# New durations and an overlap rule for the planner that orders the engines' work in a two-layer hybrid attention trunk

## The chip, the core and the metric

The kernel runs on one core of one Trainium2 chip. Its engines are TensorE (PE in the profile, with its weight loads as PEld), VectorE (DVE), ScalarE (ACT), GpSimd (POOL) and SyncE (SP), which issues nearly all transfers. Each engine takes its instructions in the order in which the program lists them and waits at an instruction until what it needs is there. The metric is the device time of one execution in microseconds: a median of 625.37 us over three runs (625.07 to 625.52) for the kernel before.

## The reference, cut to what matters

The input is 256 rows of 1024 numbers. Each of two layers normalises the rows, projects them through one matrix of 9808 columns, runs three causal attentions of 8 heads of 64 on slices of the projection, multiplies each by a SiLU gate, projects each back to 1024 channels, merges the three by sigmoid gates, projects once more and adds the residual. A last normalisation follows.

```python
for layer in range(2):
    h = rms_norm(x, gain[layer])
    proj = h @ w_in[layer]              # q, k, v, gate for a, b, c; indexer; forget; merge logits
    oa = moba(rope(qa), rope(ka), va) * silu(ga)       # one block of 256: plain causal softmax
    ob = dsa(rope(qb), rope(kb), vb, top 64 keys by the indexer) * silu(gb)
    oc = forgetting(qc, kc, vc, log_sigmoid(f)) * silu(gc)
    y = [oa @ w_branch[0], ob @ w_branch[1], oc @ w_branch[2]]
    x = x + sum(sigmoid(merge[n]) * y[n] for n in range(3)) @ w_out[layer]
out = rms_norm(x, final_gain)
```

All numbers are float32.

## The kernel before

**Tiling.** For float32 accuracy each operand of a matrix product is split into a high and a low part, and a product is three: high by high, low by high, high by low. A weight piece arrives by a transfer into one of three `raw` buffers. ACT copies it rounded into a `wh` buffer (L365), DVE writes the rest into a `wl` buffer (L369); there are six of each. `hTh` and `hTl` are the split normalised input. A projection unit (`unit_b`, `unit_y`) is 24 or 12 matmuls of 128x256 at L410, given to PE in groups of six, into one of three PSUM banks named `proj`. Units are named after their slice: `ga2` is the gate of pair 2 of attention a, `m06` a merge logit, `y04` a branch projection. A bank is free again when DVE and ACT have read it.

**Attention by pairs of heads.** Four pairs per attention. Queries are split and copied between the halves of the partitions (`qh`, `qx`, `qy`, L400 to L401 and L582); keys are written into a block layout (`bd`, L740, L742 and L744), one head in each half of the partitions. These half-height operations touch 64 partitions. Scores (L595, L597) go into two banks `s`; DVE adds the mask and takes the maximum (L656), ACT exponentiates (L660), DVE or ACT normalises (L671 or L668), PE transposes (L683), ACT and DVE split (L686, L688), PE multiplies with the values into the one bank `o` (L700 to L705), ACT and DVE add up the halves of it, again at half height (L720, L722), and gate and split the result into `og` (L725, L400, L401). In a layer the attentions run in the order a, c, b, between the projections of the gates and branches; the branch units `y0`, `y2`, `y1` read `og` of a, c and b. The output units `o00` to `o11` end the layer.

**What sets the order.** The kernel first only lists its operations, each with the operations that it depends on, the buffers that it needs, a key (its place in the layer) and a duration in nanoseconds for each engine that may run it. `Plan.run` then plays them through: it takes the engine whose next operation could start first, and of the operations that could start there at that very time the one with the lowest key, books the duration and emits it. So the order on each engine, and for some operations the engine (`normalise`, the product with the gate, the sum into `acc`), follow from the booked durations and from the delays between engines. On the chip the order is fixed; only the waits are real. Before the change a dependency over engines costs a delay from the table `LAG`, a half-height operation is booked with 18 ns (ACT copies) or 95 ns more than a full one, and DVE operations with two SBUF inputs are kept apart from GpSimd's for the whole of both.

## Time and profile before

| what | value |
|---|---|
| median of three runs | 625.37 us (625.07 to 625.52) |
| span of the profiled execution | 623.2 us |
| PE busy | 609.3 us (98%), 4808 matmuls |
| DVE busy | 537.7 us (86%) |
| ACT busy | 455.7 us (73%) |
| POOL busy | 90.2 us (14%) |
| granted TensorE clock | 0.998 |
| DMA queue q1, share of 16 engines | 52.3% |

The span is the time from the first to the last instruction of one profiled execution; the median lies 2.2 us above it. Successive matmuls overlap: the record of a matmul of 256 columns lasts 0.28 us while the next starts 0.11 us after it. A timeline row gives start, duration, engine, line, operation, tiles and, in brackets, idle time before it with the engine and tile that ended it.

### The profile page before, as it was taken

The page shows a single profiled execution, that of the slowest core. Times are in us where ns is not written, and L with a number is a line of the kernel's source. Part 1 is how long each engine was busy: PE and PEld are TensorE (multiplying, and loading weights), DVE is VectorE, ACT ScalarE, POOL GpSimd, SP SyncE. Part 2 cuts the span into 40 slices and gives each one's busy share as a digit, 9 for nine tenths or more (in the row PEclk, how much of TensorE's full clock was granted, in tenths as well). Part 3 has the DMA queues.
Part 4 walks back from the last instruction along what each step waited for, and adds up shares of the span by engine and source line. Part 5 has one row for each costly group of instructions (what it writes and reads, how often), then busy time and mean ns, then how long its engine had stood idle before and what let it go on. Part 6 is the DMA issues. An engine that isn't in the chain of part 4 may idle for free.

```text
span 623.2 us, 12650 instructions
## 1 busy us (share of the span) xinstructions
PE 609.3 (98%) x4808; PEld 583.7 (94%) x4808; DVE 537.7 (86%) x1320; ACT 455.7 (73%) x953; POOL 90.2 (14%) x98
## 2 busy tenths in 40 slices
PE   8999999999999999999999999999999999999995
PEld 7999999999998999999889999998999999999985
DVE  8899999975998789988689999998588977999683
ACT  5779499676986669955487867995689856987641
POOL 1243131000000223200005304200000013221001
PEclk9999999999999999999999999999999999999999
DMA  8945543686363653356655646447636364424831
GB/s 290 301 151 189 172 142 108 204 257 212 127 204 102 210 164 97 113 183 224 219 179 162 202 129 195 141 164 252 206 101 217 122 201 149 159 72 133 271 101 67
DMA packets 96155, 107.31 MB, mean 172 GB/s; under 512 B 4576, under 2 KB 84832, under 8 KB 96096
## 3 DMA queue, kind: packets, MB, share of 16 engines
q1 hardware_dynamic: 95808, 106.13, 52.3%
q8 instruction: 37, 0.61, 0.4%
q10 hardware_dynamic: 288, 0.39, 0.2%
q14 instruction: 22, 0.18, 0.1%
HBM read 103.37 MB, written 1.05 MB: 168 GB/s over the span
## 4 chain that ended last, share of the span: by engine, by line
PE 66%; ACT 16%; DVE 14%; issue 3%; POOL 0%; POOLq 0%; ACTq 0%
PE proj L410 57%; ACT wh L365 5%; DVE wl L369 4%; PE t L683 2%; ACT e L660 2%; ACT qx L582 2%; DVE isc L847 2%; PE proj L993 1%; DVE t L846 1%; ACT qy L582 1%; PE s L595 1%; PE s L597 1%; ACT pth L686 1%; PE t L908 1%; ACT ot L720 1%
## 5 line engine op out<-in xcount | busy, mean ns | idle before, releaser
L410 PE MATMUL proj<-hTh,wh 128*128 128x256 f32 (+1 forms) x1040 | 271.7, 279 | 2.7 <-DVE g L624 2.0
L369 DVE TENSOR_TENSOR wl<-raw,wh 128x1024 fp32r<-128x1024 f32 (+1 forms) x190 | 236.6, 1252 | 39.6 <-ACT wh L365 38.8
L410 PE MATMUL proj<-hTl,wh 128*128 128x256 f32 (+1 forms) x1040 | 270.1, 277 | 0.0
L365 ACT ACTIVATE wh<-raw 128x1024 fp32r<-128x1024 f32 (+1 forms) x190 | 199.0, 1055 | 70.9 <-PE proj L410 58.1
L410 PE MATMUL proj<-hTh,wl 128*128 128x256 f32 (+1 forms) x1040 | 235.1, 279 | 0.8 <-DVE wl L369 0.8
L410 PEld LDWEIGHTS proj<-hTh,wh 128*128 128x128 f32 (+1 forms) x1040 | 194.8, 187 | 3.8 <-DVE g L624 2.4
L410 PEld LDWEIGHTS proj<-hTl,wh 128*128 128x128 f32 (+1 forms) x1040 | 194.8, 187 | 0.3
L410 PEld LDWEIGHTS proj<-hTh,wl 128*128 128x128 f32 (+1 forms) x1040 | 175.7, 187 | 1.2 <-DVE wl L369 1.2
L460 POOL TENSOR_TENSOR rsh<-rsh,cst 128x256 f32<-128x256 f32 (+1 forms) x42 | 33.2, 790 | 384.8 <-DVE rsh L459 383.9
L462 POOL TENSOR_TENSOR rr<-rr,rsh 128x256 f32<-128x256 f32 (+1 forms) x42 | 48.9, 1166 | 10.0 <-DVE rr L461 6.2
L660 ACT ACTIVATE e<-e,st 128x128 f32<-128x128 f32 x96 | 42.6, 446 | 2.2 <-DVE st L656 2.0
L410 PE MATMUL proj<-wh,v 128*128 128x512 f32 (+1 forms) x144 | 35.5, 368 | 0.0
L410 PE MATMUL proj<-og0l,wh 128*128 128x256 f32 x128 | 33.9, 277 | 0.0
L410 PE MATMUL proj<-og0h,wh 128*128 128x256 f32 x128 | 32.6, 279 | 0.0
L410 PE MATMUL proj<-wh,hTh 128*128 128x512 f32 x80 | 31.8, 398 | 0.0
L410 PE MATMUL proj<-wh,hTl 128*128 128x512 f32 x80 | 31.3, 392 | 0.0
L410 PEld LDWEIGHTS proj<-wh,v 128*128 128x128 f32 x144 | 25.2, 188 | 4.7
L410 PE MATMUL proj<-og0h,wl 128*128 128x256 f32 x128 | 28.7, 277 | 0.0
L688 DVE TENSOR_TENSOR ptl<-t,pth 128x384 fp32r<-128x384 f32 x48 | 26.3, 554 | 0.9 <-ACT pth L686 0.4
L410 PE MATMUL proj<-wl,hTh 128*128 128x512 f32 x80 | 24.9, 391 | 0.0
L410 PEld LDWEIGHTS proj<-og0l,wh 128*128 128x128 f32 x128 | 24.0, 188 | 0.0
L410 PEld LDWEIGHTS proj<-og0h,wh 128*128 128x128 f32 x128 | 24.0, 188 | 0.0
(195 smaller groups left out, 1059.5 us busy)
## 6 DMA issues: line engine op xcount, KB each, us to landing
raw<-in_w_in_dram SPq DMA_DIRECT2D x74, 1024.0 KB, 5.0
raw<-in_w_branch_dram SPq DMA_DIRECT2D x24, 512.0 KB, 3.5
raw<-in_w_out_dram SPq DMA_DIRECT2D x8, 1024.0 KB, 7.0
tmp<-wf SPq DMA_DIRECT2D x16, 128.0 KB, 5.7
raw<-in_w_in_dram SPq DMA_DIRECT2D x3, 512.0 KB, 7.0
x<-in_x_dram SPq DMA_DIRECT2D x4, 256.0 KB, 4.5
raw<-in_w_in_dram SPq DMA_DIRECT2D x2, 320.0 KB, 6.5
out_dram<-tmp SPq DMA_DIRECT2D x2, 320.0 KB, 2.5
```

Of the source, the lines that this page charges most:

```text
L365: ACT.activation(p[0].v, sel(c.v), AF.Copy)
L369: DVE.tensor_tensor(p[1].v, sel(c.v), p[0].v.bitcast(F32), op=ALU.subtract)
L410: PE.matmul(o(), a(), b(), start=first and i == 0, stop=last and i == n - 1)
L460: gps(lambda: POOL.tensor_tensor(T(sh)[:np_], T(sh)[:np_], s[:np_], op=ALU.mult), S, [k_rope], [sh], key, "rope")
L462: gps(lambda: POOL.tensor_tensor(T(r)[:np_], T(r)[:np_], T(sh)[:np_], op=ALU.add), S, [sh], [r], key, "rope")
L582: act(lambda t=t, o=o, a=a, b=b: ACT.activation(T(t)[o], T(a)[b].bitcast(F32), AF.Copy), S, False, [a], [q[2]] if i is None else [kx[i]], ...
L595: PE.matmul(o.rearrange("p (h c) -> p h c", h=2), qh[:, sl], kl[:, :, :n], start=True, stop=False)
L597: PE.matmul(o[:, h * n:(h + 1) * n], x[h][:, sl], kh[:, 0 if shared else h, :n], start=False, stop=h == 1)
L660: act(lambda t=t, a=a, n=n, e=e, st=st: ACT.activation(T(e)[:, a:a + n], T(e)[:, a:a + n], AF.Exp, bias=T(st)[:, t:t + 1], scale=-1.0, acc ...
L683: PE.transpose(T(ps)[:, i * 128:(i + 1) * 128], T(es[h])[:, i * 128:(i + 1) * 128], ident)
L688: dve(lambda h=h, src=src: DVE.tensor_tensor(T(pl)[:, h], src(), T(ph)[:, h].bitcast(F32), op=ALU.subtract), 384, [ps, kp[h][0]], [kp[h][1 ...
L847: dve(lambda o=o, t8=t8: DVE.match_replace(o, T(t8), o, TAKEN), n, [t8], [k_isc[i]], key + r * step, "top8")
```

## The change

The planner's model is replaced; no operation of the kernel is added, removed or resized. Its parts:

- The table `LAG` and the constant `SEM` go. An operation counts as done 95 ns (ACT) or 85 ns (DVE) after the end of its booking, and another engine sees it 33 ns (POOL: 79 ns) after that, or 200 ns after its end if it ran on PE.
- A half-height operation no longer has a surcharge. Instead, neither it nor the operation after it may start before the one ahead on the same engine is done, plus 24 ns.
- A GpSimd operation is booked with 735 ns and 78 ns behind it (before 250 + 2.2 ns per column, 813 ns at 256); a DVE operation that shares its port may start 138 ns before GpSimd's end, and the other way round.
- A matmul of 256 columns is booked with 113.3 ns (114.8), of 512 with 231 ns (228); five bookings of small groups on PE are set anew.

```diff
+    def seen(d, e):
+        if d.eng == e == "PE":
+            return d.end
+        if d.eng == "SP":
+            return d.done + d.lag
+        return d.done + (1500.0 if e == "SP" else 200.0 if d.eng == "PE" else 79.0 if e == "POOL" else 33.0)
...
+                    if e in last and (o.half or last[e].half):
+                        tt = max(tt, last[e].done + STEP)
...
-                        tt = max(tt, d.end + d.lag + LAG.get((d.eng, e), 0.0 if d.eng == e else SEM) + (0.0 if d.eng == e else o.margin))
+                        tt = max(tt, self.seen(d, e) + (0.0 if d.eng == e else o.margin))
                     if e == "POOL" or (e == "DVE" and o.port):
-                        tt = max(tt, port["DVE" if e == "POOL" else "POOL"])
+                        tt = max(tt, port["DVE" if e == "POOL" else "POOL"] - 138.0)
...
+            o.done = o.end + TAIL[e]
+            last[e] = o
+            free[e] = o.end + (78.0 if e == "POOL" else 0.0)
...
 def t_pool(n):
-    return 250.0 + 2.2 * n
+    return 735.0
...
-    return 1.3 + 0.4434 * n
+    return (0.4414 if n < 512 else 0.4506) * n + 0.35
...
-            act(lambda t=t, o=o, a=a, b=b: ACT.activation(T(t)[o], T(a)[b].bitcast(F32), AF.Copy), S, False, [a],
-                [q[2]] if i is None else [kx[i]], key, name, HALF_ACT, touch=[t])
+            act(lambda t=t, o=o, a=a, b=b: ACT.activation(T(t)[o], T(a)[b].bitcast(F32), AF.Copy), S, False, [a],
+                [q[2]] if i is None else [kx[i]], key, name, touch=[t], half=True)
```

What moves: nothing in the first 37 us, and on PE nothing in the last 30 us. The order of PE's projection units stays; scores, transposes and products with the values shift between them. On SP five small row transfers of attention c (`tmp<-wf`) stand one to three places earlier, behind `fb` operations that stand earlier too. 27 operations `normalise` go from ACT to DVE and 16 from DVE to ACT, which leaves 73 of 96 on DVE instead of 62, and three products or sums go from DVE to GpSimd. In layer 0 the `wl` piece of unit `m06` is overtaken no more by 14 DVE operations that stood ahead of it (six of the top-64 search, four of rope, four `bd`), that of `m07` by 22; and the scores of the pairs a2 and a3 of layer 0 go from the units `m21` and `ga2` to the units `vc0`, the four maxima of a2 standing side by side on DVE, where a split into `og0l` and a reciprocal stood between them.

Three places follow, as the built programs list them. Lines of the changed kernel are 8 or 9 higher (L369 is L378, L624 is L633, L744 is L753).

Place one: DVE in layer 0, at the gates of the pairs b0 and b1 (`g0`, `g1`), whose banks `proj1` and `proj2` the next units need. Before:

```order
L369 TENSOR_TENSOR wl2_72<-raw1_119,wh2_65 128x1024
L401 SCALAR_TENSOR_TENSOR qy1_87<-rr0_123,qh1_81 128x256
L369 TENSOR_TENSOR wl3_73<-raw1_119,wh3_66 128x1024
L624 SCALAR_TENSOR_TENSOR g0_127<-th0_125,proj1_160 128x256
L369 TENSOR_TENSOR wl4_74<-raw2_120,wh4_67 128x1024
L624 SCALAR_TENSOR_TENSOR g1_128<-th1_126,proj2_161 128x256
L894 SCALAR_TENSOR_TENSOR mth0_151<-mth0_151,proj0_159 128x256
```

After:

```order
L378 TENSOR_TENSOR wl2_72<-raw1_119,wh2_65 128x1024
L410 SCALAR_TENSOR_TENSOR qy1_87<-rr0_123,qh1_81 128x256
L633 SCALAR_TENSOR_TENSOR g0_127<-th0_125,proj1_160 128x256
L378 TENSOR_TENSOR wl3_73<-raw1_119,wh3_66 128x1024
L633 SCALAR_TENSOR_TENSOR g1_128<-th1_126,proj2_161 128x256
L903 SCALAR_TENSOR_TENSOR mth0_151<-mth0_151,proj0_159 128x256
L378 TENSOR_TENSOR wl4_74<-raw2_120,wh4_67 128x1024
```

Each gate stands one weight split earlier, and on ACT the tanh of `g1` stands ahead of the `wh4` copy, behind which it stood. PE's order is the same here. Layer 1 shows the same pattern.

Place two: DVE in layer 0, at the key blocks of the pairs c2 (`bd1`) and c3 (`bd2`). `acc<-acc,proj0` is the first use of branch unit `y04`. Before:

```order
L369 TENSOR_TENSOR wl2_72<-raw0_118,wh2_65 128x1024
L725 TENSOR_TENSOR ot1_146<-ot1_146,g1_128 128x256
L369 TENSOR_TENSOR wl3_73<-raw1_119,wh3_66 128x1024
L401 SCALAR_TENSOR_TENSOR og1l_95<-ot1_146,og1h_94 128x256
L744 TENSOR_TENSOR bd1l_99<-proj1_160,bd1h_98 64x256 x2
L369 TENSOR_TENSOR wl4_74<-raw1_119,wh4_67 128x1024
L744 TENSOR_TENSOR bd2l_101<-proj2_161,bd2h_100 64x256 x2
L889 SCALAR_TENSOR_TENSOR acc_109<-acc_109,proj0_159 128x256
```

After:

```order
L378 TENSOR_TENSOR wl1_71<-raw2_120,wh1_64 128x1024
L378 TENSOR_TENSOR wl2_72<-raw0_118,wh2_65 128x1024
L697 TENSOR_TENSOR ptl_103<-t1_165,pth_102 128x384
L697 TENSOR_TENSOR ptl_103<-t0_164,pth_102 128x384
L753 TENSOR_TENSOR bd1l_99<-proj2_161,bd1h_98 64x256 x2
L378 TENSOR_TENSOR wl3_73<-raw1_119,wh3_66 128x1024
L665 ISA e0_131,st4_139<-s0_162,fb0_143 128x128
```

The block of c2 now stands behind the splits of pair c1's probabilities, and that of c3 (`bd2l`) has gone some 30 operations further down. Therefore PE's unit `gc2`, which follows `y05` here, gets another bank: before it is `proj2`, freed by `bd2l`, and after it is `proj0`, freed by the `acc` operation of `y04`. PE before:

```order
L410 MATMUL proj1_160<-og0l_93,wh5_68 128x256
L410 MATMUL proj1_160<-og0h_92,wl5_75 128x256 x2
L410 MATMUL proj2_161<-hTh_90,wh0_63 128x256
L410 MATMUL proj2_161<-hTl_91,wh0_63 128x256
L410 MATMUL proj2_161<-hTh_90,wh0_63 128x256
```

PE after:

```order
L419 MATMUL proj2_161<-og0l_93,wh5_68 128x256
L419 MATMUL proj2_161<-og0h_92,wl5_75 128x256 x2
L419 MATMUL proj0_159<-hTh_90,wh0_63 128x256
L419 MATMUL proj0_159<-hTl_91,wh0_63 128x256
L419 MATMUL proj0_159<-hTh_90,wh0_63 128x256
```

Place three: DVE in layer 0, at the key blocks of the pairs b2 (`bd2`) and b3 (`bd0`), which wait for rope's results `rr1` and `rr0`. Before:

```order
L461 TENSOR_TENSOR rr1_124<-proj1_160,cst_104 128x256
L459 STREAM_SHUFFLE rsh0_121<-proj2_161 128x256
L401 SCALAR_TENSOR_TENSOR og0l_93<-ot1_146,og0h_92 128x256
L461 TENSOR_TENSOR rr0_123<-proj2_161,cst_104 128x256
L894 SCALAR_TENSOR_TENSOR mth4_155<-mth4_155,proj0_159 128x256
L744 TENSOR_TENSOR bd2l_101<-rr1_124,bd2h_100 64x256 x2
L894 SCALAR_TENSOR_TENSOR mth5_156<-mth5_156,proj1_160 128x256
L896 TENSOR_TENSOR acc_109<-acc_109,mth4_155 128x256
L896 TENSOR_TENSOR acc_109<-acc_109,mth5_156 128x256
L744 TENSOR_TENSOR bd0l_97<-rr0_123,bd0h_96 64x256 x2
```

After, from `mth5` on; `rr1`, `rr0`, the split `wl0_70` and `mth4` stand just ahead of it:

```order
L903 SCALAR_TENSOR_TENSOR mth5_156<-mth5_156,proj1_160 128x256
L410 SCALAR_TENSOR_TENSOR og0l_93<-ot1_146,og0h_92 128x256
L905 TENSOR_TENSOR acc_109<-acc_109,mth4_155 128x256
L905 TENSOR_TENSOR acc_109<-acc_109,mth5_156 128x256
L378 TENSOR_TENSOR wl1_71<-raw2_120,wh1_64 128x1024
L378 TENSOR_TENSOR wl2_72<-raw2_120,wh2_65 128x1024
L633 SCALAR_TENSOR_TENSOR g2_129<-th0_125,proj2_161 128x256
L378 TENSOR_TENSOR wl3_73<-raw0_118,wh3_66 128x1024
L378 TENSOR_TENSOR wl4_74<-raw0_118,wh4_67 128x1024
L633 SCALAR_TENSOR_TENSOR g3_130<-th1_126,proj0_159 128x256
L753 TENSOR_TENSOR bd2l_101<-rr1_124,bd2h_100 64x256 x2
L753 TENSOR_TENSOR bd0l_97<-rr0_123,bd0h_96 64x256 x2
```

Five weight splits and two gates now stand ahead of both half-height pairs. On PE the work between the key unit of b3 and its scores grows from 9 groups of six matmuls to 19 (with the scores of b2 in both), and the last split into `og` of layer 1 (pair b3, read by the second half of `y10`) has four more weight splits ahead of it. The scores of a0 to a3 come later too in both layers, by one to 15 us of PE's work; in layer 0 the second halves of `y00` and `y01`, which need pair a3, move behind three groups of `gc0`.

More of the change, by code (lines that the diff above doesn't have):

```diff
@@ L34 @@
 R_RAW = 3
-LAG = {("ACT", "DVE"): 142.0, ("DVE", "ACT"): 128.0, ("DVE", "POOL"): 155.0, ("POOL", "ACT"): 75.0,
-       ("ACT", "POOL"): 75.0, ("PE", "ACT"): 197.0, ("PE", "DVE"): 196.0, ("PE", "POOL"): 200.0,
-       ("ACT", "PE"): 170.0, ("DVE", "PE"): 200.0, ("POOL", "PE"): 170.0,
-       ("DVE", "DVE"): 127.0, ("ACT", "ACT"): 127.0, ("POOL", "POOL"): 100.0, ("ACT", "SP"): 1500.0, ("DVE", "SP"): 1500.0}
-SEM = 70.0
-HALF, HALF_ACT = 95.0, 18.0
+TAIL = {"ACT": 95.0, "DVE": 85.0, "POOL": 0.0, "PE": 0.0, "SP": 0.0}
+STEP = 24.0
 SPLIT_LEAD = 2.0
@@ L110, in op @@
         o = Op()
-        o.ways, o.key, o.lag, o.name, o.margin, o.port = ways, key, lag, name, 0.0, False
+        o.ways, o.key, o.lag, o.name, o.margin, o.port, o.half = ways, key, lag, name, 0.0, False, False
         deps, o.bufs = {}, []
@@ L136, in op @@
         return o
+    @staticmethod
+    def seen(d, e):
[4 more added lines that the diff above has]
+        return d.done + (1500.0 if e == "SP" else 200.0 if d.eng == "PE" else 79.0 if e == "POOL" else 33.0)
     def run(self, slack):
-        free = {"SP": 1700.0}
+        free, last = {"SP": 1700.0}, {}
         port = {"DVE": 0.0, "POOL": 0.0}
@@ L191, in run @@
             o.eng, o.start, o.end = e, t, t + w[1]
-            free[e] = o.end
+            o.done = o.end + TAIL[e]
+            last[e] = o
+            free[e] = o.end + (78.0 if e == "POOL" else 0.0)
             if e == "POOL" or (e == "DVE" and o.port):
-                port[e] = o.end
+                port[e] = o.done
             CUR[0] = f"{o.name}|{o.n}"
@@ L201, in run @@
                 b.left -= 1
-                b.end = max(b.end, o.end + o.lag)
+                b.end = max(b.end, self.seen(o, "SP" if b.tag == "raw" else "ACT"))
                 b.users = getattr(b, "users", []) + [o.n]
                 if b.left == 0:
-                    self.tags[b.tag].append([b.end + (1500.0 if b.tag == "raw" else SEM), b.slot[1], b.users])
+                    self.tags[b.tag].append([b.end, b.slot[1], b.users])
             for q in o.out:
@@ L210, in run @@
         assert done == len(self.ops)
-        return max(o.end for o in self.ops)
+        return max(o.done for o in self.ops)
 def t_act(n, ps):
@@ L258, in pe, with act, dve @@
         return o
-    def act(fn, n, ps, reads, writes, key, name="", extra=0.0, touch=()):
-        return plan.op([("ACT", t_act(n, ps) + extra, fn)], reads, writes, key, 0.0, name, touch)
-    def dve(fn, n, reads, writes, key, name="", cost=None, touch=(), port=False):
+    def act(fn, n, ps, reads, writes, key, name="", extra=0.0, touch=(), half=False):
+        o = plan.op([("ACT", t_act(n, ps) + extra, fn)], reads, writes, key, 0.0, name, touch)
+        o.half = half
+    def dve(fn, n, reads, writes, key, name="", cost=None, touch=(), port=False, half=False):
         o = plan.op([("DVE", cost or t_dve(n), fn)], reads, writes, key, 0.0, name, touch)
-        o.port = port
-        return o
+        o.port, o.half = port, half
     def gps(fn, n, reads, writes, key, name="", cost=None):
@@ L708, in attend @@
             kv = [t for p in k_V[self.vi] for t in p]
-            pe(av, 745.0, kv + [ph, pl] + [t for h in kp for t in h], [o], key, "av", MARGIN)
+            pe(av, 705.0, kv + [ph, pl] + [t for h in kp for t in h], [o], key, "av", MARGIN)
             self.o, self.o_key = o, key
@@ L739, in write_bd @@
             if not (shared and h):
-                act(lambda hi=hi, s=s: ACT.activation(hi(), s(), AF.Copy), S, ps, [src], [toks[g][0]], key, "bd", HALF_ACT, touch=[b])
+                act(lambda hi=hi, s=s: ACT.activation(hi(), s(), AF.Copy), S, ps, [src], [toks[g][0]], key, "bd", touch=[b], half=True)
                 y = dn if x is up else up
                 act(lambda hi=hi, y=y, g=g: ACT.activation(T(b)[0][y, g], hi().bitcast(F32), AF.Copy), S, False, [toks[g][0]],
-                    [toks[g][1]], key, "bd", HALF_ACT, touch=[b])
+                    [toks[g][1]], key, "bd", touch=[b], half=True)
             dve(lambda hi=hi, lo=lo, s=s: DVE.tensor_tensor(lo(), s(), hi().bitcast(F32), op=ALU.subtract), S,
-                [src, k_bdz, toks[g][0]], [toks[h][2]], key, "bd", t_dve(S) + HALF, touch=[b], port=not ps)
+                [src, k_bdz, toks[g][0]], [toks[h][2]], key, "bd", touch=[b], port=not ps, half=True)
     def ev_kwf(l, ps, key):
```

16 lines of the change are left out of this document (8 added, 8 removed).

## The prediction

> **What bounds the kernel now.** I read the page's engine line first, then who waits for whom on PE, then the chain of waits, and last timelines around each wait.
>
> ```profile
> PE 609.3 (98%) x4808; PEld 583.7 (94%) x4808; DVE 537.7 (86%) x1320; ACT 455.7 (73%) x953; POOL 90.2 (14%) x98
> PE 66%; ACT 16%; DVE 14%; issue 3%; POOL 0%; POOLq 0%; ACTq 0%
> core 0: 623.2 us, clock 0.998
> 183.58 1.38 PE proj L410 x12
> ```
>
> PE is busy for 98% of the span at a granted clock of 0.998, and a projection's matmul of 256 columns takes it 1.38 / 12 = 0.115 us. The change alters no matmul and moves no projection unit against another, so PE's work stays and only PE's waits can be won. These are PE's own waits, all but the two at the start of the program (`t` and L993), where no operation moves:
>
> ```profile
> PE proj L410 <- DVE g L624: 2.0, 2, 1.0
> PE s L595 <- DVE st L656: 1.2, 2, 0.8
> PE proj L410 <- DVE wl L369: 0.8, 2, 0.5
> PE proj L410 <- DVE bd2l L744: 0.4, 1, 0.4
> PE proj L410 <- DVE bd0l L744: 0.4, 1, 0.4
> PE s L595 <- DVE bd1l L744: 0.2, 1, 0.2
> PE s L595 <- DVE bd2l L744: 0.2, 1, 0.2
> ```
>
> Ten waits, 5.2 us, each ended by DVE. They cost more than that, because the wait is counted from the modelled end of the last matmul, and without it the next would have started before that end:
>
> ```profile
> 85.33 0.28 PE L410 MATMUL proj<-hTl,wh 128*128 128x256 f32 x1
> 86.08 0.39 PE L410 MATMUL proj<-hTh,wl 128*128 128x256 f32 x1 [0.48 <-DVE wl L369]
> ```
>
> From start to start 0.75 us, of which 0.115 is the matmul: 0.64 lost, 0.16 more than the 0.48 shown. So the ten cost 5.2 + 10 x 0.16 = **6.8 us**. That is the whole stake. The chain's 30% on ACT and DVE is no second reserve: it runs through those engines while PE is busy with other units.
>
> **The change part by part.**
>
> The two gates, 2.0 + 2 x 0.16 = 2.3 us. The wait in layer 0:
>
> ```profile
> 215.91 0.42 DVE L624 SCALAR_TENSOR_TENSOR g<-th,proj 128x256 f32<-128x256 f32 x1 [0.95 <-ACT th L623]
> 215.90 0.42 ACT L582 ACTIVATE qy<-qh 64x256 fp32r<-64x256 f32 x1
> 216.34 1.06 ACT L365 ACTIVATE wh<-raw 128x1024 fp32r<-128x1024 f32 x1
> 217.30 0.36 ACT L623 ACTIVATE th<-proj 128x256 f32<-128x256 f32 x1
> 217.43 1.23 DVE L369 TENSOR_TENSOR wl<-raw,wh 128x1024 fp32r<-128x1024 f32 x1 [1.10 <-ACT wh L365]
> 218.57 0.42 DVE L624 SCALAR_TENSOR_TENSOR g<-th,proj 128x256 f32<-128x256 f32 x1
> 217.67 0.39 PE L410 MATMUL proj<-og1h,wl 128*128 128x256 f32 x2
> 219.04 0.39 PE L410 MATMUL proj<-hTh,wh 128*128 128x256 f32 x1 [0.98 <-DVE g L624]
> ```
>
> PE could go on at 217.67 + 2 x 0.115 = 217.90, but its bank is freed by `g1` at 218.99. `g1` waited for a `wl` split of 1.23, and that for a `wh` copy of 1.06 ahead of the tanh. In the new order (place one) the tanh takes the copy's slot at 216.34 and ends by 216.7; `wl4` stands behind `g1`, and `wl3` between the gates. At worst `g0` stays at 215.91, `wl3` runs behind it until 217.4 and `g1` until 217.8, and PE's 217.90 is just met. The copy that loses its slot is for a weight read several units later. Gain 2.3.
>
> The two weight splits, 0.8 + 0.32 = 1.1 us, both in layer 0.
>
> ```profile
> 79.10 1.52 DVE L369 TENSOR_TENSOR wl<-raw,wh 128x1024 fp32r<-128x1024 f32 x1
> ```
>
> PE waits for its end at 80.62. Fourteen operations that were ahead of it stand behind it now; four half-height writes alone are 4 x 0.43 = 1.7 us (0.86 a pair, below), more than the 0.45 it was late. `m07`'s split loses 22. Gain 1.1. Late instead is the top-64 search, which only attention b needs, at 230 us.
>
> The two score banks, 1.2 + 0.32 = 1.5 us: the next pair's scores waited for the third of four maxima, behind a split into `og`. The maxima stand together now, and in layer 0 the next scores follow three more groups on PE. Gain 1.5.
>
> The four waits for key blocks, 1.2 + 0.64 = 1.8 us (place two). Half of it, the bank of `gc2`, goes for certain: that bank is now freed by the `acc` operation of `y04`, with `y05` between. The other half is that c2's scores wait for its blocks:
>
> ```profile
> 176.31 0.77 ACT L740 ACTIVATE bd1h<-proj 64x256 fp32r<-64x256 f32 x2
> 176.98 0.84 ACT L742 ACTIVATE bd1h<-bd1h 64x256 fp32r<-64x256 f32 x2
> 177.00 0.42 DVE L401 SCALAR_TENSOR_TENSOR og1l<-ot,og1h 128x256 fp32r<-128x256 f32 x1
> 177.34 0.85 DVE L744 TENSOR_TENSOR bd1l<-proj,bd1h 64x256 fp32r<-64x256 f32 x2
> 180.20 0.86 DVE L744 TENSOR_TENSOR bd2l<-proj,bd2h 64x256 fp32r<-64x256 f32 x2
> 181.09 0.42 DVE L889 SCALAR_TENSOR_TENSOR acc<-acc,proj 128x256 f32<-128x256 f32 x1
> ```
>
> From the first ACT copy to the last DVE write 178.19 - 176.31 = 1.9 us, with 0.2 after PE 2.1.
>
> What the change adds. At c0 and c2, in both layers, PE has four groups of six matmuls between the key unit's end and the pair's scores, 4 x 0.69 = 2.8 us, where the chain of 2.1 must fit. If ACT takes the copies at once nothing is lost. With one weight copy of 1.06 ahead of them it takes 3.2 and costs 0.4, with two 4.2 and 1.5. Four places: 0 to 6.0 us. I take one copy at each, 4 x 0.4 = **1.7 us**, since the weight copies are what ACT mostly has ready.
>
> Moves between engines. DVE gets 11 operations `normalise` more, ACT 11 fewer, GpSimd three products.
>
> ```profile
> L671 DVE TENSOR_SCALAR e<-e,st 128x256 f32<-128x256 f32 x30 | 10.5, 350 | 0.0
> L668 ACT ACTIVATE e<-e,st 128x256 f32<-128x256 f32 x18 | 9.1, 504 | 0.5 <-DVE st L664 0.2
> L725 DVE TENSOR_TENSOR ot<-ot,g 128x256 f32<-128x256 f32 x24 | 10.1, 419 | 0.2
> L462 POOL TENSOR_TENSOR rr<-rr,rsh 128x256 f32<-128x256 f32 x40 | 46.6, 1166 | 9.8 <-DVE rr L461 6.2 <-DVE selb L850 1.3
> 50.00:100.00 50.00, 49.24 (x425) 48.60 (x424) 48.78 (x157) 40.99 (x92) 15.04 (x15) 1.00 0.51 161
> 350.00:400.00 50.00, 49.90 (x438) 49.54 (x437) 49.11 (x158) 38.98 (x83) 12.43 (x13) 1.00 0.52 164
> ```
>
> DVE: 11 x 0.35 - 3 x 0.42 = 2.6 us more on 537.7; ACT: 11 x 0.50 = 5.5 us less; GpSimd, busy for 14%, three times 1.2 at most, each with a weight split beside it on DVE. The windows (columns PE, PEld, DVE, ACT, POOL busy) show DVE full in two stretches of 50 us; there each us is paid by what stands last on DVE, the search. Cover: the search has over 100 us to spare. Without it DVE's 2.6 would come in full. Cost 0, bound 2.6. SP's five moved transfers wait for operations that moved ahead with them: 0.
>
> Sum against the profiled span: 623.2 - 2.3 - 1.1 - 1.5 - 1.8 + 1.7 = 618.2. The median of the runs is 2.2 above the span: **620.4 us**.
>
> A rule weighed. The planner lets a half-height operation overlap neither neighbour. In the rows the pair on DVE starts at 177.34, 0.08 before the operation ahead ends (177.42), and only behind a pair there is a gap (181.06 to 181.09). The Trainium skill, "VectorE: DVE Perf Modes", section "Two Vector instructions with no wait between them", says that an operation is held back when its operands start in another group of 32 partitions than those before it, not when it is half height; by that only the second half and the operation behind a pair are held, and the rows agree. By it the planner books 0.11 us too much for each of 50 pairs on DVE; alone that is idle time in a plan and none on the chip, so the sum stays.
>
> **The rivals.**
>
> All waits go and none come: 625.4 - 6.8 = 618.6. For it: the 2.1 us chain fits into 2.8 when ACT is free, and ACT gets 5.5 us less to do. Against it: an order in which PE never waits would be new for this kernel.
>
> The waits only change place: the upper bound of 6.0 holds, 625.4 - 6.8 + 6.0 = 624.6. For it: the same engines feed PE, and DVE is full in two stretches. Against it: those stretches end with work that PE doesn't wait for.
>
> Slower, because half-height operations are put off. A candidate that must wait out the 24 ns always starts later than a full one, so the planner takes every ready full operation first, whatever its key. Place three shows five splits in front of b2's and b3's blocks. PE has other units meanwhile, but none at the end of an attention, where a branch unit needs the last pair.
>
> ```profile
> 575.35 0.42 DVE L401 SCALAR_TENSOR_TENSOR og0l<-ot,og0h 128x256 fp32r<-128x256 f32 x1
> 574.21 1.22 DVE L369 TENSOR_TENSOR wl<-raw,wh 128x1024 fp32r<-128x1024 f32 x1
> 584.01 0.28 PE L410 MATMUL proj<-og0h,wh 128*128 128x256 f32 x1
> ```
>
> Pair b3's last split ends at 575.8, the second half of `y10` starts at 584.0: 8.2 us of cover. Four more splits ahead of it cost 4 x 1.13 = 4.5. It decides from a delay of 8.2 on. If the five splits ahead of the blocks come in full as well, the delay is 9 x 1.13 = 10.2, 2.0 too long; at the ends of a and b in both layers that is 4 x 2.0 = 8.0: 625.4 - 6.8 + 1.7 + 8.0 = 628.3. Against it: the five and the four are mostly the same prefetch, counted twice.
>
> **How the numbers follow.** The forecast (some waits return) 0.60, all gone 0.18, waits elsewhere 0.11, slower 0.11. A measurement of this kernel tells some 0.2% from no change, 1.25 us. Faster by more than that is below 624.1: forecast and all gone, 0.78. Within it lies the third case, whose 624.6 is inside by a little, 0.11; slower 0.11. The range leaves out most of the slower case and a little below all gone (small gaps under 0.15 us may close as well): 617.6 to 625.2.
>
> **What would show it.** In the changed kernel's list of waits on PE, `g` should be gone, `wl` gone or at the start only, `st` gone. New rows should be small and of the kind `s <- bd` or `s <- qx`. DVE's busy time should rise by some 2 to 3 us and ACT's fall by 4 to 6. The scores of a2 should start near 117 us instead of 99, with PE busy throughout. The prediction is wrong if PE's waits sum to more than 3 us, if a wait for `og` shows at `y00` or `y10`, or if the time moves with PE's waits unchanged.

## The result, and the profile after

| | median | range | span of the profiled execution | clock |
|---|---|---|---|---|
| before (same batch) | 625.22 us | 625.00 to 625.52 | 623.2 us | 0.998 |
| changed | 621.01 us | 620.42 to 621.37 | 619.3 us | 0.999 |

The ratio is 0.9931, with a 95% interval of 0.9917 to 0.9945: 4.2 us faster, where 5.0 were forecast, and 0.6 us above the predicted 620.4.

The engine line and the shares of the chain of waits, on the page of the changed kernel:

```profile
PE 609.2 (98%) x4808; PEld 582.9 (94%) x4808; DVE 536.5 (87%) x1328; ACT 448.4 (72%) x942; POOL 93.8 (15%) x101
PE 81%; DVE 9%; ACT 6%; issue 2%; POOL 1%; DMA 1%; SPq 0%; POOLq 0%; DVEq 0%
```

PE's work is what it was (609.3 before), and its share of the chain rises from 66% to 81%. The list of PE's waits in the changed kernel (total, times, longest), without the start of the program:

```profile
PE s L604 <- ACT tmp L825: 0.5, 2, 0.4
PE t L801 <- DVE fz L795: 0.5, 1, 0.5
PE s L604 <- DVE bd2l L753: 0.3, 1, 0.3
PE s L604 <- DVE st L665: 0.2, 1, 0.2
```

All ten waits that the prediction priced are gone, 5.2 us of listed idle; 1.5 us is new. Where they lay is seen when the span is cut into four stretches. The columns are the stretch, its length, busy time of PE, PEld, DVE, ACT and POOL with the instructions, clock, DMA share and GB/s. Before:

```profile
30.00:100.00 70.00, 69.24 (x599) 68.51 (x598) 68.73 (x193) 56.56 (x117) 23.44 (x23) 1.00 0.52 165
100.00:330.00 230.00, 228.05 (x1751) 216.32 (x1750) 193.83 (x446) 168.51 (x354) 18.52 (x20) 1.00 0.54 175
330.00:430.00 100.00, 99.00 (x819) 96.22 (x818) 96.94 (x266) 79.13 (x168) 24.77 (x26) 1.00 0.52 167
430.00:600.00 170.00, 168.47 (x1395) 164.03 (x1394) 142.99 (x339) 125.66 (x264) 16.96 (x17) 1.00 0.51 169
```

Changed:

```profile
30.00:100.00 70.00, 69.38 (x596) 68.14 (x595) 66.92 (x192) 54.59 (x113) 23.05 (x23) 1.00 0.56 167
100.00:330.00 230.00, 230.00 (x1777) 218.72 (x1777) 197.48 (x460) 167.94 (x355) 21.33 (x23) 1.00 0.56 177
330.00:430.00 100.00, 98.91 (x803) 94.96 (x802) 93.99 (x260) 78.25 (x166) 25.27 (x24) 1.00 0.54 164
430.00:600.00 170.00, 170.00 (x1404) 165.70 (x1403) 144.85 (x343) 124.02 (x262) 17.08 (x18) 1.00 0.53 168
```

From 100 to 330 us and from 430 to 600 PE no longer waits at all. In the stretch between, where DVE runs the indexer, the search and rope of layer 1, PE is idle for 1.1 us as it was for 1.0, and from 30 to 100 us for 0.6 as it was for 0.8: there the waits that went were replaced by others.

**The gaps counted.** The listed idle leaves out part of each wait, as the prediction said. So I took the distance from the start of each matmul to the start of the next, subtracted the median distance for a matmul of that width, and summed what is over 150 ns. After the first 20 us this gives 7.2 us in 12 gaps before and 3.6 us in 11 gaps after. These 3.5 us, of 3.9 in the span, are the gain. By stretches it is 2.6 us that went between 100 and 330 us and 2.0 behind 430, while the gaps grew from 1.1 to 1.3 us before 100 us and from 1.4 to 2.3 between 330 and 430.

**Place one, the gates.** Timeline of layer 0 in the changed kernel, at the gates of b0 and b1:

```profile
212.21 0.41 DVE L633 SCALAR_TENSOR_TENSOR g<-th,proj 128x256 f32<-128x256 f32 x1
212.87 1.23 DVE L378 TENSOR_TENSOR wl<-raw,wh 128x1024 fp32r<-128x1024 f32 x1 [0.25 <-ACT wh L374]
213.96 0.38 ACT L632 ACTIVATE th<-proj 128x256 f32<-128x256 f32 x1
214.36 1.06 ACT L374 ACTIVATE wh<-raw 128x1024 fp32r<-128x1024 f32 x1
214.37 0.42 DVE L633 SCALAR_TENSOR_TENSOR g<-th,proj 128x256 f32<-128x256 f32 x1 [0.27 <-ACT th L632]
216.25 0.39 PE L419 MATMUL proj<-og1h,wl 128*128 128x256 f32 x2
216.47 0.28 PE L419 MATMUL proj<-hTh,wh 128*128 128x256 f32 x1
```

The tanh now runs ahead of the weight copy, the second gate ends at 214.79, and the unit that needs its bank starts at 216.47, two matmuls of 0.11 behind 216.25. There are 1.7 us to spare where before 1.15 were lost.

**The new waits.** A little over half of them, 1.9 of 3.6 us, have two causes. The first is in the preparation of attention b: the indexer's scores go into the two banks `s` in turn, and a bank is free when ACT has read it (`tmp`, L824 and L825). Timeline at 47 us:

```profile
47.17 0.37 ACT L824 ACTIVATE tmp<-s 128x256 f32<-128x256 f32 x1
47.57 0.42 ACT L591 ACTIVATE qy<-qh 64x256 fp32r<-64x256 f32 x1
47.89 0.57 ACT L825 ACTIVATE tmp<-s 128x512 f32<-128x512 f32 x1
47.87 0.28 PE L606 MATMUL s<-bd0h,qy 128*128 128x128 f32 x1
48.52 0.50 PE L604 MATMUL s<-bd0l,qh 128*128 128x512 f32 x1 [0.37 <-ACT tmp L825]
```

A half-height query copy stands between the two reads, the second read ends at 48.46, and PE starts 0.65 us after its last matmul instead of 0.11. This costs 0.53, 0.25 and 0.37 us at three places. The second: the forget gate's small sums (`fz`, five short DVE operations one after the other) stand between steps of the search in layer 1:

```profile
361.24 0.16 DVE L794 TENSOR_TENSOR fz<-fz 128x16 f32<-128x16 f32 x1
361.32 0.08 DVE L856 MATCH_VALUE_LOAD isc<-t,isc 128x8 f32 x1
361.40 0.40 DVE L856 MATCH_REPLACE8 isc<-t,isc 128x256 f32<-128x256 f32 x1
361.72 0.16 DVE L795 SCALAR_TENSOR_TENSOR fz<-fz 128x16 f32<-128x16 f32 x1
361.93 0.39 PE L801 MATMUL t<-fz,cst 128*128 128x8 f32 x2 [0.46 <-DVE fz L795]
```

That is 0.63 us here and 0.17 in layer 0. The rest are scores of attention a that wait for their block or for the second bank (1.0 us in three), and 0.7 us in three gaps at transposes and products.

### The profile page after: what moved, and what is told of

Its sections match the earlier page's. It is cut to its first block, busy times and chain, and to the rows that moved or that the text cites. A ratio compares the mean times of both kernels' runs of the same rounds, so it can differ in the third digit from the quotient of the medians.

```text
span 619.3 us, 12624 instructions
## 1 busy us (share of the span) xinstructions
PE 609.2 (98%) x4808; PEld 582.9 (94%) x4808; DVE 536.5 (87%) x1328; ACT 448.4 (72%) x942; POOL 93.8 (15%) x101
## 4 chain that ended last, share of the span: by engine, by line
PE 81%; DVE 9%; ACT 6%; issue 2%; POOL 1%; DMA 1%; SPq 0%; POOLq 0%; DVEq 0%
PE proj L419 71%; DVE wl L378 3%; PE t L692 2%; ACT wh L374 2%; PE s L604 2%; PE s L606 1%; PE proj L1002 1%; PE o L710 1%; PE o L714 1%; ACT qx L591 1%; DVE isc L856 1%; DVE rsh L468 1%; DMA raw<-in_w_in_dram 1%; DVE t L855 1%; ACT e L669 1%
## 5 line engine op out<-in xcount | busy, mean ns | idle before, releaser
L378 DVE TENSOR_TENSOR wl<-raw,wh 128x1024 fp32r<-128x1024 f32 (+1 forms) x190 | 235.6, 1249 | 36.5 <-ACT wh L374 35.7
L471 POOL TENSOR_TENSOR rr<-rr,rsh 128x256 f32<-128x256 f32 (+1 forms) x42 | 52.5, 1253 | 8.4 <-DVE rr L470 5.7
L697 DVE TENSOR_TENSOR ptl<-t,pth 128x384 fp32r<-128x384 f32 x48 | 24.9, 548 | 1.0 <-ACT pth L695 0.9
L872 ACT ACTIVATE mth<-proj 128x256 f32<-128x256 f32 x32 | 11.9, 378 | 16.9 <-PE proj L419 16.4
```

The source lines that it names most:

```text
L378: DVE.tensor_tensor(p[1].v, sel(c.v), p[0].v.bitcast(F32), op=ALU.subtract)
L471: gps(lambda: POOL.tensor_tensor(T(r)[:np_], T(r)[:np_], T(sh)[:np_], op=ALU.add), S, [sh], [r], key, "rope")
L697: dve(lambda h=h, src=src: DVE.tensor_tensor(T(pl)[:, h], src(), T(ph)[:, h].bitcast(F32), op=ALU.subtract), 384, [ps, kp[h][0]], [kp[h][1 ...
L872: act(lambda: ACT.activation(T(th), T(ps)[:, :S], AF.Tanh, scale=0.5), S, True, [ps], [th], u - EARLY, "mth")
```

## The experiments

Twelve kernels. "Gaps" is the sum just defined, at the start (first 20 us) and later. "Late" compares the planner's own start times with the trace: for each operation of ACT or DVE planned between 30 and 590 us, its start in the trace minus its start in the plan, less the same difference of PE's work at that moment; the mean is shown. It says how far an engine runs behind the plan in relation to PE.

| kernel | median us | span us | gaps, start + later | span less gaps | ACT late ns | DVE late ns |
|---|---|---|---|---|---|---|
| change without the half-height rule | 628.15 | 626.3 | 2.1 + 8.4 | 615.8 | 373 | 359 |
| before, rule on DVE alone | 627.09 | 625.2 | 2.6 + 8.5 | 614.2 | 256 | 140 |
| before, nudged | 625.58 | 623.6 | 2.5 + 7.6 | 613.5 | 236 | 181 |
| before | 625.2 to 625.4 | 623.2 | 2.1 + 7.2 | 614.0 | 202 | 188 |
| before, 127 ns for half height | 623.04 | 621.0 | 2.2 + 5.6 | 613.2 | 48 | 81 |
| change, 8 ns more everywhere | 622.57 | 620.7 | 2.9 + 4.0 | 613.8 | -12 | -6 |
| change with the old delays | 622.38 | 620.5 | 3.0 + 4.3 | 613.2 | 76 | 73 |
| before, rule on ACT alone | 622.18 | 620.3 | 2.6 + 4.3 | 613.5 | 74 | 207 |
| before, time spread evenly | 622.08 | 620.2 | 4.1 + 3.6 | 612.5 | 39 | 59 |
| **change** | 621.01 | 619.3 | 2.3 + 3.6 | 613.4 | 142 | 144 |
| before with the half-height rule | 620.73 | 619.1 | 3.4 + 2.8 | 612.9 | 17 | 0 |
| change, nudged | 620.01 | 617.5 | 2.2 + 2.6 | 612.7 | 70 | 101 |
| change with GpSimd's old lock | 619.04 | 616.9 | 2.7 + 2.4 | 611.8 | 16 | 46 |
| change with the old GpSimd bookings | 618.31 | 616.5 | 2.1 + 2.1 | 612.3 | -21 | -26 |

Two things stand in this table. The span less PE's gaps is 612 to 614 us for all but one: most of the difference in time is what PE waits, as the prediction took it. And the four kernels in which ACT and DVE together run furthest behind the plan are the four with the most gaps (7.2 to 8.5 us after the start). Below that, lateness sorts the kernels poorly: in five of the ten others (127 ns, 8 ns more, the old delays, the rule on ACT alone, time spread evenly) the two engines together are less late than in the change, and PE waits as long or longer. Over all fourteen the rank correlation of lateness and later gaps is 0.78, over the ten without those four 0.43.

**Which part of the change carries the gain.** First the half-height rule is undone in the changed kernel.

```diff
-                    if e in last and (o.half or last[e].half):
-                        tt = max(tt, last[e].done + STEP)
...
+        extra += (95.0 if name == "og" else 18.0) if half else 0.0
...
-        o = plan.op([("DVE", cost or t_dve(n), fn)], reads, writes, key, 0.0, name, touch)
+        o = plan.op([("DVE", (cost or t_dve(n)) + (95.0 if half else 0.0), fn)], reads, writes, key, 0.0, name, touch)
```

> The changed planner with the half-height rule alone undone (old surcharges of 95 and 18 ns back, no gap of 24 ns). In its order the gates of b0 and b1 still stand one weight split earlier and the splits of m06 and m07 still stand ahead of the search, but gc2 again takes the bank that a half-height bd write frees, and b2's blocks have two more weight splits ahead of them than before the change instead of five. Theory H (the half-height rule carries the gain): gates and wl go (-3.4), the waits on bd stay, about 623.0 us (622.3 to 623.8). Rival R (the new delays and the GpSimd bookings carry it, the half-height rule only shifts work): as the changed kernel, 621.0 within 0.6. Rival P (putting half-height work off costs time): below 620.3.

Measured: 628.15 us, ratio 1.0045 (1.003 to 1.006). It is 7.1 us above the change, not 2, and slower than before. PE's waits there:

```profile
PE s L603 <- DVE st L664: 2.4, 3, 1.3
PE t L691 <- ACT e L676: 1.3, 3, 0.5
PE s L603 <- ACT tmp L823: 1.3, 2, 0.7
```

How they come about shows at the longest, in the timeline of that kernel:

```profile
83.44 0.69 DVE L409 SCALAR_TENSOR_TENSOR qy<-rr,qh 128x256 fp32r<-128x256 f32 x1 [0.40 <-ACT qh L408]
84.06 0.28 DVE L664 CUSTOM_DVE_ANT_0 e<-s,cst 128x128 f32<-128x128 f32 x1
84.82 0.08 DVE L664 DVE_READ_ACCUMULATOR2_ANT st<- 128x1 f32 x1
83.35 0.28 PE L418 MATMUL proj<-hTl,wh 128*128 128x256 f32 x1
84.95 0.39 PE L603 MATMUL s<-bd2l,qh 128*128 128x256 f32 x1 [1.33 <-DVE st L664]
```

DVE is held at `qy` for 0.40 us because ACT is late with `qh`, and `qy` takes 0.69 us instead of 0.42 beside a GpSimd operation (83.12 to 83.86). The four maxima stand behind `qy` in the fixed order, and PE starts 0.05 us after the third of them is written (84.90). In this kernel ACT and DVE run 0.37 and 0.36 us behind the plan, where before they ran 0.20 and 0.19. The likely reason, not tested by itself, is that with 18 ns for a half-height copy the plan gives ACT too little time, and that the new delays take away a reserve that the old ones held. Then the rule alone is put into the kernel before:

```diff
+                    if e in last and (o.half or last[e].half):
+                        tt = max(tt, last[e].done + STEP)
...
-HALF, HALF_ACT = 95.0, 18.0
+TAIL = {"ACT": 95.0, "DVE": 85.0, "POOL": 0.0, "PE": 0.0, "SP": 0.0}
+STEP = 24.0
```

> The kernel before with the half-height rule alone added; delays, GpSimd and PE bookings as before the change. Its order has all the moves that the prediction priced: gates earlier, splits of m06 and m07 earlier, maxima of a2 side by side, gc2 in the bank of y04; b2's blocks have seven more weight splits ahead. Theory H: about 621.3 us (620.6 to 622.2). Rival R: 623.5 or more, since the delays are still the old ones. Rival P: also 623 or more, with waits on bd or og at PE.

Measured: 620.73 us, ratio 0.9925 (0.991 to 0.9939). The rule alone brings the whole gain; ACT and DVE start where the plan has them (17 and 0 ns late).

**The other two parts.** The bookings of GpSimd go back to the old form, then, in another kernel, the delays:

```diff
-                        tt = max(tt, port["DVE" if e == "POOL" else "POOL"] - 138.0)
+                        tt = max(tt, port["DVE" if e == "POOL" else "POOL"])
...
-            free[e] = o.end + (78.0 if e == "POOL" else 0.0)
+            free[e] = o.end
...
-                port[e] = o.done
+                port[e] = o.end
...
-    return 735.0
+    return 250.0 + 2.2 * n
```

> The changed planner with the bookings of GpSimd undone (813 ns an operation, DVE operations with two SBUF inputs kept apart for the whole of it, no 78 ns behind). Theory H: no difference that counts, 621.0 within 0.9. Rival G (the lock's booking carries the gain): 623 or more, with the rope results late and PE waiting for scores.

Measured: 618.31 us, ratio 0.9886 (0.9871 to 0.9901), 2.7 us faster than the change and the fastest kernel of all. Both expectations missed.

```diff
-        if d.eng == e == "PE":
-            return d.end
-        if d.eng == "SP":
-            return d.done + d.lag
-        return d.done + (1500.0 if e == "SP" else 200.0 if d.eng == "PE" else 79.0 if e == "POOL" else 33.0)
+        return d.end + d.lag + LAG.get((d.eng, e), 0.0 if d.eng == e else SEM)
...
-                b.end = max(b.end, self.seen(o, "SP" if b.tag == "raw" else "ACT"))
+                b.end = max(b.end, o.end + o.lag + (1500.0 if b.tag == "raw" else SEM))
```

> The changed planner with the old table of delays between engines; half-height rule, GpSimd and PE bookings as changed. Theory H: no difference that counts, 621.0 within 0.9. Rival D (the delays carry the gain): 623 or more, PE's waits back at gates and score banks.

Measured: 622.38 us, ratio 0.9954 (0.9937 to 0.997): the new delays bring 1.4 us beside the rule, a little outside what was expected. With the old GpSimd bookings they bring 2.4 (620.73 to 618.31), together with the new bookings on PE, which were not tried alone.

**The rule on one engine.** In the kernel before, ACT follows the rule and DVE keeps its surcharge, and the other way round:

```diff
+                    if e == "ACT" and e in last and (o.half or last[e].half):
+                        tt = max(tt, last[e].done + STEP)
```

> The kernel before with the half-height rule on ACT alone (DVE keeps the surcharge of 95 ns). Of the sites that the prediction priced, its order has the gates' and the weight splits' (2.3 + 1.1 us), not the key blocks' bank and not the maxima. Theory T (each site's fix is worth its term, wherever the rest of the order goes): 625.4 - 3.4 = 622.0 us, 621.0 to 623.5, and no wait for g on PE. Theory S (any redrawing of the order moves the time by some 2 us at random, the sites mean little): anywhere from 619 to 629. Theory R (only the rule on both engines together helps, since half a rule leaves the plan as wrong as before): 625 or more.

Measured: 622.18 us, ratio 0.9954 (0.9939 to 0.9968), 0.2 off what the terms gave, but by another sum. No wait for `g` is left; those for the key blocks have gone too, although the bank of `gc2` is the old one, likely since ACT's copies come closer to where the plan has them (ACT 74 ns late in place of 202). So all ten gaps are gone, and two smaller ones with them, 7.2 us in all, and 4.3 are new. Its two largest waits:

```profile
PE t L797 <- DVE fz L791: 1.5, 1, 1.5
PE s L600 <- DVE st L661: 0.8, 1, 0.8
```

> The kernel before with the half-height rule on DVE alone (ACT keeps its surcharges of 18 and 95 ns). Its order has the weight splits', the maxima's and the key blocks' sites in the new form (1.1 + 1.5 + 1.8 us), and the gates in the old one (one weight split more ahead of g). Theory T: 625.4 - 4.4 = 621.0 us without new waits, 622.7 with the 1.7 of the prediction; PE still waits about 2.0 us for g. Theory S: anywhere from 619 to 629. Theory R: 625 or more.

Measured: 627.09 us, ratio 1.0031 (1.002 to 1.0043), slower than before although three of the four sites are in their new form; the sum over sites is off by at least 4.4 us. The waits:

```profile
PE proj L416 <- ACT acc L866: 1.9, 2, 1.3
PE s L601 <- DVE st L662: 1.0, 2, 0.5
PE proj L416 <- DVE qy L407: 0.9, 1, 0.9
PE proj L416 <- DVE g L630: 0.9, 2, 0.4
```

The waits of the sites that the prediction priced shrink or go here too (`g` by half), but others are larger. The longest:

```profile
390.01 1.06 ACT L371 ACTIVATE wh<-raw 128x1024 fp32r<-128x1024 f32 x1 [1.56 <-PE proj L416]
390.97 0.37 ACT L866 ACTIVATE acc<-proj 128x256 f32<-128x256 f32 x1
391.39 0.39 PE L416 MATMUL proj<-hTh,wh 128*128 128x256 f32 x1 [1.30 <-ACT acc L866]
```

ACT stands idle at a weight copy whose buffer PE has not yet given back; the sum into `acc` stands behind the copy, and PE waits for the bank that the sum frees. A sum over sites cannot see this: it takes away waits of the old order and knows nothing of the new one.

**How far a redrawing of the order goes by itself.** Every DVE operation is booked 2 ns longer, in the kernel before and in the changed one:

```diff
-    return 68.0 + n / 0.96
+    return 70.0 + n / 0.96
```

> The kernel before with every DVE operation booked 2 ns longer (0.5%), which means nothing for the chip but redraws the order: 36 of 848 groups on PE, 138 of 1143 operations on DVE and 84 of 844 on ACT change their place; the gates, the key blocks' bank and the scores of a2 stay as in the kernel before, the maxima get the new form. Theory T: 625.4 less at most 1.5 for the maxima: 623.9 to 625.9. Theory S: over 1.5 us away from 625.4 with a chance of a half, to either side.

> The changed kernel with every DVE operation booked 2 ns longer: 33 of 848 groups on PE, 93 of 1151 operations on DVE and 60 of 833 on ACT change their place, all priced sites as in the changed kernel. Theory T: 621.0, within 1.0. Theory S: over 1.5 us away from 621.0 with a chance of a half, to either side; if so, the 2.7 us that the GpSimd bookings seemed to cost and the 1.4 that the delays seemed to bring are no more than such a redrawing.

Measured: 625.58 us, ratio 1.0004 (0.9995 to 1.0013), and 620.01 us, ratio 0.9914 (0.9899 to 0.9929). About a tenth of DVE's operations stand elsewhere and the time moves by 0.2 and by 1.0. The gain of the rule (4.6 to 7.1 us) is far outside that, the delays' 1.4 to 2.4 somewhat; what differs by 1 us between two orders says nothing. Two redrawings are few, so 1.0 is the larger of two values and no bound.

**Is it the form of the rule, or the time that it books?** In the trace of before, neighbours on an engine that have nothing to wait for overlap by 96 ns on ACT and 83 ns on DVE (medians). Where one of the two is at half height, 256 of 313 neighbours on ACT start only after the end of the one ahead, and 101 of 140 on DVE. Against the overlap of two full ones that adds up to 30.5 us on ACT, where the surcharges book 8.1 (196 x 18 and 48 x 95 ns), and to 11.1 us on DVE, where they book 9.5 (100 x 95 ns). So the kernel before was short of 22 us of booking on ACT and about right on DVE.

Two kernels book this time without the rule. In the one the two surcharges become 127 ns, which is what the rule cost the plan for each half-height operation; in the other the same sum is spread over all operations.

```diff
-HALF, HALF_ACT = 95.0, 18.0
+HALF, HALF_ACT = 127.0, 127.0
...
```

> The kernel before with one number in place of two: each half-height operation is booked 127 ns longer than a full one (before 18 or 95 on ACT, 95 on DVE). 127 ns is what the half-height rule cost the plan for each such operation (30.9 us of forced gaps for 244 operations on ACT, 12.6 us for 100 on DVE), but here as a duration, so that an operation may start behind it at once. Theory M (what counts is that the plan gives ACT and DVE the time that they need; in the runs so far the time follows how late ACT and DVE run behind the plan: 0.37 us in the run of 628.2, 0.2 in that of 625.4, 0.0 in that of 620.7): 621.5 us, within 1.5. Theory F (what counts is the form of the rule, by which half-height operations are put behind full ones and stand in rows): 625, within 1; the order has the bank of gc2 and the scores of a2 as in the kernel before.

Measured: 623.04 us, ratio 0.9969 (0.9957 to 0.998), between the two theories and just outside the range of each.

```diff
-    return (51.0 if ps else 94.0) + n / 1.2
+    return (78.0 if ps else 121.0) + n / 1.2
...
-    return 68.0 + n / 0.96
+    return 71.0 + n / 0.96
```

> The kernel before with the same time in total, spread over all operations: every operation of ACT is booked 27 ns longer and every one of DVE 3 ns. Theory M in its plainest form (the sum alone counts): 621.5, within 1.5. Theory M' (the time must stand at the operations that take it): 623 to 625, since chains of half-height operations stay too short in the plan. Theory F: 625, within 1.

Measured: 622.08 us, ratio 0.9956 (0.9939 to 0.9972), though its gaps in the first 20 us are 2.1 us larger than before, since the new bookings shift operations there too. So the time booked, without any rule of overlap, gives 2.1 and 3.1 of the rule's 4.6 us, and against M' it does not have to stand at the operations that take it; the 1 us between the two kernels is within a redrawing. The remaining 1.5 to 2.5 us may be the form's; with redrawings of up to 1.0 that part is not settled.

**Is a reserve what the old GpSimd bookings gave?** The changed kernel with 8 ns more for every operation of ACT and DVE:

```diff
-    return 68.0 + n / 0.96
+    return 76.0 + n / 0.96
...
-    return (51.0 if ps else 94.0) + n / 1.2
+    return (59.0 if ps else 102.0) + n / 1.2
```

> The changed kernel with every operation of ACT and DVE booked 8 ns longer (some 6.7 us more on ACT, 9 on DVE). In the changed kernel ACT and DVE start 0.14 us later against PE than planned, in the version with the old GpSimd bookings 0.02 us earlier, and that one took 2.7 us less. Theory M (the old GpSimd bookings helped as a reserve on DVE): 618.5 to 620.0. Theory G (they helped since GpSimd's lock itself is right in the old form, so a reserve elsewhere is worth nothing): 621.0, within 1.0. Either way more than 622 would say that a reserve costs more than it brings.

Measured: 622.57 us, ratio 0.9961 (0.9946 to 0.9975), 1.6 us above the change; its gaps are 0.6 us larger at the start and 0.4 later. Both theories missed: more than 622 was to say that a reserve costs more than it brings. ACT and DVE are on time in it (-12 and -6 ns), and nothing is won. A general reserve is not it, and being on time is not enough. Last, the lock alone goes back:

```diff
-                        tt = max(tt, port["DVE" if e == "POOL" else "POOL"] - 138.0)
+                        tt = max(tt, port["DVE" if e == "POOL" else "POOL"])
...
-                port[e] = o.done
+                port[e] = o.end
```

> The changed kernel with GpSimd's lock as before: operations that share the port are kept apart in full, with no start 138 ns early; GpSimd's durations stay new (735 ns, 78 ns behind). Theory L (the 138 ns are what cost 2.7 us, since operations of DVE that are planned into GpSimd's end stand there and run longer): 618.3, within 1.0. Theory D (the shorter duration cost it): 621.0, within 1.0. Theory S (a redrawing of the order that happened to fall well): anything from 619.5 to 622.5.

Measured: 619.04 us, ratio 0.9903 (0.9887 to 0.992): 2.0 of the 2.7 us, within what the theory of the lock gave and 0.5 below the range of S. The groups of the indexer's sum, which reads two SBUF tiles and which the planner therefore keeps apart from GpSimd, with mean ns behind the busy time, in the changed kernel, in that with the old lock, and in that with all old bookings:

```profile
L835 DVE SCALAR_TENSOR_TENSOR isc<-tmp,widx,isc 128x128 f32<-128x128 f32 (+1 forms) x28 | 12.3, 492 | 0.0
```

```profile
L835 DVE SCALAR_TENSOR_TENSOR isc<-tmp,widx,isc 128x128 f32<-128x128 f32 (+1 forms) x28 | 11.4, 462 | 0.2 <-ACT tmp L825 0.2
```

```profile
L835 DVE SCALAR_TENSOR_TENSOR isc<-tmp,widx,isc 128x128 f32<-128x128 f32 (+1 forms) x28 | 10.6, 430 | 1.3 <-ACT tmp L825 0.8 <-ACT tmp L824 0.5
```

The mean falls from 492 to 462 and 430 ns. By their records, 8 of the 28 sums overlap an operation of GpSimd in the changed kernel, 5 with the old lock and 2 with all old bookings; in the changed kernel those 8 last 685 ns on average, the other 20 last 415. The total of DVE operations with two SBUF inputs that overlap GpSimd stays (63, 62 and 61). Over all fourteen traces 6 to 11 sums overlap in the five kernels that plan with the 138 ns, 0 to 7 in the nine that do not. So the 138 ns tend to move the meetings into the indexer's stretch, where 1.15 of the change's 3.6 us of new gaps lie. But the nudged change (620.01) and the old lock (619.04) are no further apart than one redrawing, so the lock's 2 us are likely, not shown.

## Why the prediction was right

**The stake.** Right. The ten waits were to cost 6.8 us; the ten gaps add up to 6.7 (with two smaller ones of 0.2 and 0.3 that the list does not show, 7.2). The terms by the gaps: gates 2.3 (said 2.3), weight splits 1.1 (1.1), score banks 1.5 (1.5), key blocks 1.8 (1.8). All are gone.

**Whether the order does it.** A site's price is right, but it is won only if no other wait comes. The rule on ACT alone met its forecast of two terms (3.2 of 3.4 us) with all ten gaps gone and 4.3 us new; the rule on DVE alone has three sites in the new form and is 1.7 us slower than before. The runs point to something that the prediction did not weigh: whether the plan gives each engine the time that it needs. The booked time alone brought 2.1 and 3.1 us; that it is the whole cause is not shown.

**What the change adds.** The step that was mis-sized: +1.7 us was said, the new gaps are 3.6. The place was wrong as well. c0 and c2 were to pay with their 2.1 us chain in 2.8 us of cover; their scores lie between 100 and 330 and behind 430 us, where PE does not wait. The new waits are at the indexer's banks, `fz` and the scores of attention a. The prediction searched for new waits at the sites that it had seen move, and its bounds (0 to 6.0) held for the sum only by their width. (4 x 0.4 is 1.6 and not 1.7, which changes nothing.) That the forecast came within 0.6 us all the same is partly luck: against 1.9 us too little for the new gaps stand the 0.5 us of the two small gaps, which the sum left out, and 0.5 us by which the span outside the gaps fell, whose cause is open.

**The signs.** The "no more than 3 us" of listed idle holds: 1.5 beside the start. `g` and `wl` are gone as said, and the scores of a2 start at 115.3 us, about the 117 that were said, with PE busy. `st` is not gone, 0.2 us of it stands at 85 us; and the new rows are mostly `s <- tmp` and `t <- fz`, not `s <- bd` or `s <- qx`.

**Moves between engines.** Cost 0 is not contradicted. DVE's busy time did not rise by 2 to 3 us, it fell by 1.2 (537.7 to 536.5). The 11 more normalisations are there, as the groups of the changed kernel show (40 + 33 on DVE):

```profile
L680 DVE TENSOR_SCALAR e<-e,st 128x256 f32<-128x256 f32 x40 | 13.7, 348 | 0.4
L680 DVE TENSOR_SCALAR e<-e,st 128x128 f32<-128x128 f32 x33 | 9.6, 290 | 0.2
```

By the sum of the records they add 3.5 us. But rope's `qy` (-2.2) and the forget gate's `fz` (-2.0) are shorter: 8 of 24 `qy` overlap a GpSimd operation where 11 did, and 3 of 20 `fz` where 8 did. The sums into `acc` take 1.0 less, since two of them are on GpSimd now. The prediction left out that a DVE operation's length depends on what GpSimd does beside it. ACT fell by 7.3 us, where 4 to 6 were said.

**GpSimd's bookings and the delays.** The prediction priced neither as a part of its own. In these orders the first cost 1.7 to 2.7 us (620.73 to 622.38 with the old delays, where the bookings on PE differ too; 618.31 to 621.01 with the new), the second brought 1.4 to 2.4. That they nearly cancel is luck.

**The rule weighed.** The prediction held that 0.11 us too much for each of 50 pairs on DVE is idle time in a plan and costs nothing on the chip. The runs do not speak against it, and go further: time booked at operations that did not need it helped (the spread booking, 3.1 us), where it made up for time needed and not booked. That half height is not what holds an operation back, as the prediction argued against the planner's rule, is borne out by the counts in the last section. The Trainium skill, "SBUF — State Buffer", section "SBUF: two separate sides", says that the port which DVE and GpSimd share is locked for a whole instruction. By that the old lock is right and the 138 ns are not. The records agree as to the hold: the low part of a query, computed behind a GpSimd operation, took 0.96 us instead of 0.42,

```profile
340.68 0.96 DVE L406 TENSOR_TENSOR qy<-rr,qh 128x256 fp32r<-128x256 f32 x1
339.76 1.60 POOL L471 TENSOR_TENSOR rr<-rr,rsh 128x256 f32<-128x256 f32 x1
```

and 341.64 - 0.42 = 341.22 is 0.14 before GpSimd's record ends at 341.36. Over the 37 operations of the changed kernel that are stretched so, the median is 0.139 us. So the 138 ns are a true number of the records, and planning with it still did not pay; why is open.

**The rivals.** "All waits go" would have been right for the kernel with the old GpSimd bookings (618.3 against 618.6), which has 2.1 us of gaps left. "The waits only change place" holds up to 100 us and from 330 to 430, where the gaps even grew. "Slower, since half-height operations are put off": no wait for `og` at `y00` or `y10` appears in any list of the runs that have the rule, and in the changed kernel none shows from start to start. The lists leave out small ones, though: in the kernel with the old GpSimd bookings two matmuls of `y00` start 0.23 and 0.35 us late, at 137.00 and 137.46, each 0.05 us after `og0h` and `og0l` are written (136.95 and 137.41). That is 0.6 us of this rival in the fastest kernel. The two kernels that were slower than before show no such wait; in both, ACT's half-height copies are booked with 18 ns more, and ACT runs 0.26 and 0.37 us behind the plan.

## What to carry to other kernels

Where a planner sets the order and TensorE is 98% busy, compare the plan's start times with a trace engine by engine before tuning anything else: the four kernels furthest behind their plan waited longest here, though closer to the plan lateness no longer told which order was better. Look first at the engine that is shortest of booked time: the rule on ACT, which was 22 us short, won 3.2 us alone, and on DVE alone, with ACT still short, it lost 1.7 us. And nudge a constant that means nothing before believing any difference: here one of two redrawings of the order was worth 1.0 us, a quarter of the gain.

## What the runs showed of the hardware

The largest surprise is the length of short DVE operations beside GpSimd: the same indexer sum has a mean of 410 to 511 ns from order to order over the fourteen traces, and `qy` took 0.42 or 0.96 us, with no change of the work. Where none of the 28 sums overlaps GpSimd (the spread booking) the mean is 410; a sum that does overlap lasts 649 to 870 ns on average, by trace. The number of DVE operations with two SBUF inputs that overlap GpSimd is 59 to 81 in a trace; which operations they are changes with the order. The other is where a half-height operation costs time. By its record a copy of 64x256 on ACT is hardly longer than a full read of 128x256 (0.42 and 0.37 us in the rows at 47 us), so 18 ns seemed enough; the cost lies in the lost overlap between neighbours, 30.5 us for 244 operations on ACT, 125 ns each. It is not a matter of height: in those rows the full read behind the copy starts at 47.89, 0.10 before the copy ends, and 57 of the 313 neighbours overlap.

What tells them apart in these traces is where the operands start. In the built kernel every operand of ACT and DVE starts at partition 0 or 64. Take the operations in the trace of before that start no later than 60 ns after the end of the one ahead (without those behind an accumulator read, and without the search). Ask of each whether an input starts at another partition than the input last read from the same memory (SBUF or PSUM), or its output at another than the output last written there. On ACT all 259 with such a change start only after the end of the one ahead, and of the 318 without it 299 overlap that one by more than 40 ns. In the changed kernel it is 239 of 239, and 306 of 321. On DVE before it is 100 of 100, and 699 of 725. So half height is a stand-in for a change of the starting partition: of ACT's 308 half-height neighbours sorted so, 248 have the change and 60 do not; 52 of these overlap, although the rule books a gap for them. What planning by the starting partition would bring was not tried.
